# Gate and up projections of a hybrid decoder block: most 512-column matmuls become pairs of 256 columns

## The chip, the cores and the metric

The kernel runs on one core of one Trainium2 chip. The metric is the device time of one execution in microseconds (us). Its engines are called PE (TensorE, the matmuls), DVE (VectorE), ACT (ScalarE), POOL (GpSimd) and SP (SyncE, which issues the DMAs here); PEld is PE's weight load, which overlaps its matmuls.

## The reference

One layer of a decoder block with D = 2048, 256 tokens and a hidden width of 5632. Four token mixers share an input and an output projection; behind them comes a gated feed-forward part with a short causal convolution over the gate. The change lies in the first half of that part, the two projections by `w_gate` and `w_up`:

```python
def conv_ffn(h, w_gate, w_up, conv_w, conv_b, w_down):
    gate = causal_dwconv(h @ w_gate, conv_w) + conv_b
    return (jax.nn.silu(gate) * (h @ w_up)) @ w_down
...
        h = rmsnorm(x, norm_ffn[l]) * (1.0 + sc2) + sh2
        x = x + g2 * conv_ffn(h, ffn_w_gate[l], ffn_w_up[l], ffn_conv_w[l], ffn_conv_b[l], ffn_w_down[l])
```

All of it is float32.

## The kernel before

The kernel computes a float32 product as three products of fp32r parts. Each operand is split into a high part (the value rounded to fp32r) and a low part (what is left): `x w` becomes `xh wh + xl wh + xh wl`. The weights are split as they arrive. `load` (L153) brings a piece of 128 x 1024 values by one DMA on SP's queue into `wr` (five buffers), and `load_split` (L158) makes `wh` by a cast on ACT (L115) and `wl` by a subtraction on DVE (L116, recorded at L100), three buffers of each. All matmuls go through `mm` (L97).

The order of the program is: the modulation vectors and the input projection (tiles `acc` and `ext`), the mixers (`gdt`, `oxt`), the output projection (`wot`), then the feed-forward part (`fpt`). One form of the earlier stages is spoken of below: in the input projection, `gdn` uses each weight tile twice, once with the 256 columns of the high half of the activations and once with the 256 of the low half, both into the same columns of `acc`, and then the `wl` tile with the high half.

In the feed-forward part the normalized activations stand in `H2` (a buffer named `bigA` in the profile): for each of the 16 K tiles of 128 rows, 512 columns, of which the first 256 are the high half of the 256 tokens and the last 256 the low half. `proj` (L1026) makes 512 output features of the gate or of the up projection. It takes four banks of PSUM from the pool `fpp`, which has eight, one bank for each column tile of 128 features, and goes over the 16 K tiles in eight loads of two. For each K tile there are four matmuls of 512 columns (`wh` of a column tile with both halves of `H2`; the sum with the high half arrives in the bank's columns 0 to 255, that with the low half in 256 to 511) and four of 256 columns (`wl` with the high half, added into columns 0 to 255). At the end ACT copies the second half of each bank to `lo` (L1040), and DVE adds it to the first half in place (L1041).

The loop at L1045 calls `proj` for the gate and for up, 11 times each, so there are 88 loads for the gate and 88 for up. The results stay in PSUM; behind each pair, ACT and DVE apply the convolution, the SiLU and the product, and split the result into `AH` and `AL`. From these the down projection is made, with `AH` and `AL` as the weights and the pieces of `w_down` as what streams, in chunks of 512 and 256 columns.

The instructions of each engine are put in order by a scheduler that works ahead of time with an own simulation of the engines. So the order on PE is not quite that of the source: at the start of a gate projection, where banks of PSUM come free one by one, it goes by column tile over several K tiles, and the 512- and 256-column matmuls come in pairs or alternate.

Of the kernel before, what the change touches and what calls it, by code (L numbers as in the profile page):

```python
# [8 lines left out]
F32 = mybir.dt.float32  # L9
# [3 lines left out]
ALU = mybir.AluOpType  # L13
# [3 lines left out]
P = 128  # L17
D = 2048
KT = D // P
T = 256  # L20
# [53 lines left out]
def trunk_kernel(ctx: ExitStack, tc: tile.TileContext, x, c, w_mod, b_mod, norm_mix, norm_ffn, w_in,  # L74
# [4 lines left out]
    V, S_, G, PE = nc.vector, nc.scalar, nc.gpsimd, nc.tensor  # L79
# [16 lines left out]
    def mm(o, l, r, start=True, stop=True):  # L96
        PE.matmul(o, lhsT=l, rhs=r, start=start, stop=stop, skip_group_check=True)  # L97

    def tt(o, a, b, op):
        V.tensor_tensor(out=o, in0=a, in1=b, op=op)  # L100
# [57 lines left out]
    def load_split(view, k0, nk, c0, n):  # L158
        wr = load(view, k0, nk, c0, n)
        wh = wp.tile([P, 1024], F32R, name="wh", tag="wh", bufs=3).rearrange("p (k n) -> p k n", n=n)  # L160
        wl = wp.tile([P, 1024], F32R, name="wl", tag="wl", bufs=3).rearrange("p (k n) -> p k n", n=n)
        split(wh[:, 0:nk], wl[:, 0:nk], wr[:, 0:nk])
        return wh, wl
# [64 lines left out]
    with ExitStack() as ph:  # L228
# [59 lines left out]
        with ExitStack() as st:  # L288
# [19 lines left out]
            b = ext()  # L308
            PE.transpose(b[:, 0:KT], crow, ident[:KT, :KT])
            act(cond, b[:, 0:KT], AF.Silu)  # L310
            b = ext()
# [11 lines left out]
            for k in range(0, KT, 2):  # L323
                b = ext().rearrange("p (k t) -> p k t", t=T)
# [653 lines left out]
        with tc.tile_pool(name="op", bufs=2, reuse_waits="tile") as op:  # L978
            for n, (c0, w) in enumerate(chunks):
                ns, gs = slice(c0, c0 + w), slice(c0 % 1024, c0 % 1024 + w)  # L980
                a = a0
                if n > 0:
                    a = [wop.tile([P, 512], F32, name="wot", tag="wot")[:, 0:w] for _ in range(NT)]
# [8 lines left out]
    with ExitStack() as ph:  # L992
        fpp = ph.enter_context(tc.tile_pool(name="fpp", bufs=8, space=PSUM, reuse_waits="tile"))
        fpt = lambda: fpp.tile([P, 512], F32, name="fpt", tag="fpt")
        H2 = bigA()
        with tc.tile_pool(name="hp", bufs=2, reuse_waits="tile") as hp:
# [9 lines left out]
            for k in range(0, KT, 2):  # L1006
                b = fpt().rearrange("p (k t) -> p k t", t=T)
# [17 lines left out]

        def proj(gp, view, c0):  # L1026

            a = [fpt() for _ in range(4)]
            for g in range(KT // 2):
                wh, wl = load_split(view, 2 * g, 2, c0, 512)  # L1030
                for kk in range(2):
                    k = 2 * g + kk
                    fs = lambda f: slice(f * P, f * P + P)
                    for f in range(4):
                        mm(a[f], wh[:, kk, fs(f)], H2[:, k], start=k == 0, stop=False)
                    for f in range(4):
                        mm(a[f][:, 0:T], wl[:, kk, fs(f)], H2[:, k, 0:T], start=False, stop=k == KT - 1)
            for b in a:
                lo = gp.tile([P, T], F32, name="lo", tag="lo")
                S_.copy(lo, b[:, T:])  # L1040
                tt(b[:, 0:T], b[:, 0:T], lo, ALU.add)  # L1041
            return [b[:, 0:T] for b in a]

        with tc.tile_pool(name="gp", bufs=2, reuse_waits="tile") as gp:
            for n in range(NF // 4):  # L1045
                gt = proj(gp, wg_v, 512 * n)
                ut = proj(gp, wu_v, 512 * n)
                for i in range(4):
                    f = 4 * n + i
                    w3 = lambda j: V3[:, j * NF + f:j * NF + f + 1]  # L1050
                    cv = gp.tile([P, T], F32, name="cv2", tag="cv2")
                    act(cv, gt[i], AF.Identity, scale=w3(2), bias=CB[:, f:f + 1])
                    for sh in (1, 2):
                        stt(cv[:, sh:], gt[i][:, 0:T - sh], w3(2 - sh), cv[:, sh:], ALU.mult, ALU.add)
                    act(cv, cv, AF.Silu)
                    tt(cv, ut[i], cv, ALU.mult)
                    split(AH[:, f], AL[:, f], cv)
# [4 lines left out]
        with tc.tile_pool(name="op2", bufs=1, reuse_waits="tile") as op:  # L1062
            chunks = ((0, 512), (512, 512), (1024, 512), (1536, 256), (1792, 256))
            fs = op.tile([P, NT, len(chunks)], F32, name="fs")
            f1 = op.tile([P, 4], F32, name="f1")
            for n, (c0, w) in enumerate(chunks):
# [3 lines left out]
                a = [fpt()[:, 0:w] for _ in range(NT)]  # L1070
                nk = 1024 // w
                for g in range(NF // nk):
                    wh, wl = load_split(wd_v, nk * g, nk, c0, w)
                    for kk in range(nk):
                        k = nk * g + kk
# [55 lines left out]
```

## Time and profile before

| | |
|---|---|
| time, median of 3 runs | 1303.85 us (1300.9 to 1304.77) |
| profiled execution: its time | 1303.01 us |
| profiled execution: span of the core | 1301.2 us |
| mean granted TensorE clock | 0.985 |
| PE busy | 1248.5 us, 7927 matmuls |
| PEld busy | 1091.0 us |
| DVE busy | 891.0 us |
| ACT busy | 636.7 us |

The time is that of the execution as the device reports it, the span the distance from the first to the last instruction in the trace. Where an engine is named with a tile (`fpt<-bigA,wh`), the tile written stands ahead of the arrow and the tiles read behind it. The shape behind that is partitions x columns. "128*128" is the part of the array in use. In a row of groups, busy time and the mean of one instruction follow, then the idle time of the engine just before them and what ended it. In a row of the timeline the first number is the start in us from the start of the span, the second the length of the row, and xN the number of instructions that were merged in it.

### The profile page before, as it was taken

The page shows a single profiled execution, that of the slowest core. Times are in us where ns is not written, and L with a number is a line of the kernel's source. Part 1 is how long each engine was busy: PE and PEld are TensorE (multiplying, and loading weights), DVE is VectorE, ACT ScalarE, POOL GpSimd, SP SyncE. Part 2 cuts the span into 40 slices and gives each one's busy share as a digit, 9 for nine tenths or more (in the row PEclk, how much of TensorE's full clock was granted, in tenths as well). Part 3 has the DMA queues.
Part 4 walks back from the last instruction along what each step waited for, and adds up shares of the span by engine and source line. Part 5 has one row for each costly group of instructions (what it writes and reads, how often), then busy time and mean ns, then how long its engine had stood idle before and what let it go on. Part 6 is the DMA issues. An engine that isn't in the chain of part 4 may idle for free.

```text
span 1301.2 us, 20372 instructions
## 1 busy us (share of the span) xinstructions
PE 1248.5 (96%) x7927; PEld 1091.0 (84%) x7927; DVE 891.0 (68%) x1201; ACT 636.7 (49%) x1000; POOL 22.7 (2%) x31
## 2 busy tenths in 40 slices
PE   2799999999999999999999999999999999999996
PEld 1799999898876788888888888888888888888896
DVE  7689797989763397676656656665656597964543
ACT  3455344774354454564545555554555454443432
POOL 0200000010000100000000000000000000000000
PEclk9799999999999999999999999999999999999998
DMA  9999998796566988556576666666665699875652
GB/s 321 277 367 378 337 341 290 259 339 212 164 236 240 318 317 276 156 165 192 163 214 190 186 187 193 190 172 206 187 187 163 219 374 359 323 243 194 192 181 81
DMA packets 174231, 311.94 MB, mean 240 GB/s; under 512 B 16172, under 2 KB 65331, under 8 KB 173495
## 3 DMA queue, kind: packets, MB, share of 16 engines
q1 hardware_dynamic: 174135, 310.65, 72.9%
q8 instruction: 62, 1.02, 0.3%
q14 instruction: 34, 0.28, 0.1%
HBM read 308.51 MB, written 2.10 MB: 239 GB/s over the span
## 4 chain that ended last, share of the span: by engine, by line
PE 92%; DMA 4%; SPq 1%; DVE 1%; ACT 1%; issue 1%; POOLq 0%; ACTq 0%; DVEq 0%
PE fpt L97 57%; PE ext L97 16%; PE wot L97 5%; PE gdt L97 4%; PE acc L97 4%; PE bgt L97 3%; DMA wm<-in_w_mod_dram 3%; PE oxt L97 2%; DMA wr<-in_w_in_dram 1%; DVE ga L103 1%; DMA ct<-in_cst_dram 0%; ACT xT L1011 0%; DVE wl L100 0%; SPq L399 0%; SPq L155 0%
## 5 line engine op out<-in xcount | busy, mean ns | idle before, releaser
L100 DVE TENSOR_TENSOR wl<-wr,wh 128x1024 fp32r<-128x1024 f32 x384 | 469.2, 1223 | 293.6 <-ACT wh L115 292.6
L115 ACT CAST wh<-wr 128x1024 fp32r<-128x1024 f32 x384 | 403.4, 1051 | 494.9 <-PE fpt L97 310.8
L97 PE MATMUL fpt<-bigA,wh 128*128 128x512 f32 x1408 | 399.6, 395 | 2.1 <-DVE bigA L103 2.1
L97 PEld LDWEIGHTS fpt<-bigA,wh 128*128 128x128 f32 x1408 | 239.3, 189 | 32.8 <-issue 2.2
L97 PEld LDWEIGHTS fpt<-bigA,wl 128*128 128x128 f32 x1408 | 222.4, 188 | 34.4 <-DVE wl L100 3.6
L97 PE MATMUL fpt<-bigA,wl 128*128 128x256 f32 x1408 | 240.4, 279 | 0.0
L103 DVE SCALAR_TENSOR_TENSOR ga<-wm,cond,ga 128x1024 f32<-128x1024 f32 x139 | 177.8, 1279 | 9.5 <-DMA wm<-in_w_mod_dram 8.6
L97 PE MATMUL fpt<-wl,AH 128*128 128x512 f32 (+1 forms) x440 | 152.9, 348 | 0.0
L97 PE MATMUL fpt<-wh,AL 128*128 128x512 f32 (+1 forms) x440 | 152.5, 347 | 0.0
L97 PE MATMUL fpt<-wh,AH 128*128 128x512 f32 (+1 forms) x440 | 142.5, 348 | 0.0
L97 PE MATMUL ext<-bigA,wh 128*128 128x256 f32 x768 | 137.0, 280 | 0.0
L97 PEld LDWEIGHTS ext<-bigA,wh 128*128 128x128 f32 x768 | 117.3, 188 | 3.1 <-DVE dS L100 0.8
L97 PE MATMUL ext<-bigA,wl 128*128 128x256 f32 x384 | 107.2, 280 | 1.7 <-DVE wl L100 1.7
L97 PEld LDWEIGHTS fpt<-wh,AH 128*128 128x128 f32 x440 | 83.3, 189 | 10.7 <-issue 0.2
L97 PEld LDWEIGHTS fpt<-wh,AL 128*128 128x128 f32 x440 | 83.3, 189 | 10.5 <-issue 0.2
L97 PEld LDWEIGHTS fpt<-wl,AH 128*128 128x128 f32 x440 | 83.3, 189 | 10.5 <-issue 0.2
L97 PE MATMUL acc<-bigA,wh 128*128 128x256 f32 x384 | 70.3, 289 | 4.7 <-ACT bigA L115 2.9
L97 PEld LDWEIGHTS ext<-bigA,wl 128*128 128x128 f32 x384 | 72.1, 188 | 3.0 <-DVE wl L100 2.1
L97 PE MATMUL ext<-wh,bigA 128*128 128x256 f32 (+1 forms) x320 | 68.0, 304 | 0.0
L97 PEld LDWEIGHTS acc<-bigA,wh 128*128 128x128 f32 x384 | 60.7, 198 | 5.1 <-ACT bigA L115 3.0
L97 PE MATMUL wot<-wh,bigA 128*128 128x512 f32 (+1 forms) x256 | 63.2, 337 | 0.0
L97 PEld LDWEIGHTS ext<-wh,bigA 128*128 128x128 f32 x320 | 51.7, 188 | 5.5 <-ACT wh L115 1.7
(340 smaller groups left out, 1191.9 us busy)
## 6 DMA issues: line engine op xcount, KB each, us to landing
wm<-in_w_mod_dram SPq DMA_DIRECT2D x192, 512.0 KB, 5.8
wr<-in_w_in_dram SPq DMA_DIRECT2D x88, 512.0 KB, 9.7
wr<-in_ffn_w_gate_dram SPq DMA_DIRECT2D x88, 512.0 KB, 3.9
wr<-in_ffn_w_up_dram SPq DMA_DIRECT2D x88, 512.0 KB, 4.4
wr<-in_ffn_w_down_dram SPq DMA_DIRECT2D x88, 512.0 KB, 4.5
wr<-in_w_out_dram SPq DMA_DIRECT2D x32, 512.0 KB, 4.2
xt<-in_x_dram SPq DMA_DIRECT2D x2, 1024.0 KB, 7.2
bigC<-in_x_dram SPq DMA_DIRECT2D x2, 1024.0 KB, 8.6
```

The lines of the kernel that those rows point to most:

```text
L97: PE.matmul(o, lhsT=l, rhs=r, start=start, stop=stop, skip_group_check=True)
L100: V.tensor_tensor(out=o, in0=a, in1=b, op=op)
L103: V.scalar_tensor_tensor(out=o, in0=a, scalar=s, in1=b, op0=op0, op1=op1)
L115: S_.copy(hi, src)
```

## The change

`proj` alone changes. In each load of two K tiles only column tile 0 of the first K tile keeps its matmul of 512 columns. Every other `wh` tile is used in two matmuls of 256 columns, one with the high and one with the low half of `H2`, and both add into columns 0 to 255 of the bank. The matmuls with `wl` stay as they are. So only the bank of column tile 0 has anything in its second half, and only that bank is followed by the copy to `lo` and the add.

```diff
             a = [fpt() for _ in range(4)]
             for g in range(KT // 2):
                 wh, wl = load_split(view, 2 * g, 2, c0, 512)
                 for kk in range(2):
                     k = 2 * g + kk
                     fs = lambda f: slice(f * P, f * P + P)
                     for f in range(4):
-                        mm(a[f], wh[:, kk, fs(f)], H2[:, k], start=k == 0, stop=False)
+                        if f == 0 and kk == 0:
+                            mm(a[f], wh[:, kk, fs(f)], H2[:, k], start=k == 0, stop=False)
+                        else:
+                            mm(a[f][:, 0:T], wh[:, kk, fs(f)], H2[:, k, 0:T], start=k == 0, stop=False)
+                            mm(a[f][:, 0:T], wh[:, kk, fs(f)], H2[:, k, T:], start=False, stop=False)
                     for f in range(4):
                         mm(a[f][:, 0:T], wl[:, kk, fs(f)], H2[:, k, 0:T], start=False, stop=k == KT - 1)
-            for b in a:
-                lo = gp.tile([P, T], F32, name="lo", tag="lo")
-                S_.copy(lo, b[:, T:])
-                tt(b[:, 0:T], b[:, 0:T], lo, ALU.add)
+            lo = gp.tile([P, T], F32, name="lo", tag="lo")
+            S_.copy(lo, a[0][:, T:])
+            tt(a[0][:, 0:T], a[0][:, 0:T], lo, ALU.add)
             return [b[:, 0:T] for b in a]
```

## The prediction

> **What bounds the kernel now.** First the page: busy time by engine, then the chain that ended last by engine and line.
>
> ```profile
> span 1301.2 us, 20372 instructions
> ...
> PE 1248.5 (96%) x7927; PEld 1091.0 (84%) x7927; DVE 891.0 (68%) x1201; ACT 636.7 (49%) x1000; POOL 22.7 (2%) x31
> ...
> PE 92%; DMA 4%; SPq 1%; DVE 1%; ACT 1%; issue 1%; POOLq 0%; ACTq 0%; DVEq 0%
> ```
>
> PE carries 92% of the chain. The chain in order of time shows that gate and up and the down projection after them are one unbroken stretch of PE:
>
> ```profile
> 549.25 738.94 PE fpt L97 x4141
> ```
>
> So in gate and up only what changes PE's own pace, or makes PE wait, moves the end. The groups by line and shape of that stage (549 to 1042 us):
>
> ```profile
> L97 PE MATMUL fpt<-bigA,wh 128*128 128x512 f32 x1408 | 399.6, 395 | 2.1 <-DVE bigA L103 2.1
> L97 PE MATMUL fpt<-bigA,wl 128*128 128x256 f32 x1408 | 240.4, 279 | 0.0
> L97 PEld LDWEIGHTS fpt<-bigA,wh 128*128 128x128 f32 x1408 | 239.3, 189 | 32.8 <-issue 2.2
> L97 PEld LDWEIGHTS fpt<-bigA,wl 128*128 128x128 f32 x1408 | 222.4, 188 | 34.4 <-DVE wl L100 3.6
> L100 DVE TENSOR_TENSOR wl<-wr,wh 128x1024 fp32r<-128x1024 f32 x175 | 214.1, 1224 | 175.3 <-ACT wh L115 175.3
> L115 ACT CAST wh<-wr 128x1024 fp32r<-128x1024 f32 x176 | 184.6, 1049 | 198.7 <-PE fpt L97 188.1 <-ACT bigA L112 5.5 <-issue 2.6
> ```
>
> Three things are seen here. There is one weight load for each matmul. PE's waits sum to some 8 us of 493, 2.1 of them the start of the stage. And ACT waits 188 us for PE to free a `wh` buffer, which is what a bound PE looks like from the other side. A mean of 395 ns is not the pace: matmuls overlap, and the pace is the distance of their starts. That is read from the timeline of PE, here a clean stretch of ten K tiles:
>
> ```profile
> 620.52 1.09 PE L97 MATMUL fpt<-bigA,wh 128*128 128x512 f32 x4
> 621.45 0.62 PE L97 MATMUL fpt<-bigA,wl 128*128 128x256 f32 x4
> 621.91 1.09 PE L97 MATMUL fpt<-bigA,wh 128*128 128x512 f32 x4
> 622.84 0.62 PE L97 MATMUL fpt<-bigA,wl 128*128 128x256 f32 x4
> ...
> 634.39 1.09 PE L97 MATMUL fpt<-bigA,wh 128*128 128x512 f32 x4
> ```
>
> From 620.52 to 634.39 are ten K tiles: 1.387 us each. The four 512-column matmuls take 0.93 of it (232.5 ns each), the four 256-column ones 0.45 to 0.46 (0.457 by difference, 114 ns each). Two of 256 columns cost 228 ns, less than one of 512. This is the core of the case, since the change trades the one for the other.
>
> **What the change does, part by part.** There are 88 + 88 loads of two K tiles. In each, one of eight 512-column matmuls stays and seven become two 256-column ones with the same weights: 1232 matmuls of 512 columns go, 2464 of 256 come, and with them 1232 more weight loads, as each matmul has its own. Columns streamed are the same. A load's block on PE is now 2 x 1.387 = 2.774 us. Afterwards it is one 512-column matmul and 14 + 8 = 22 of 256.
>
> The price of a 256-column matmul in such a long row is the unknown. The trace of before has rows of the very form in the input projection (`wh` with the high half, `wh` again with the low half, then `wl`, into the same columns), and they do not agree:
>
> ```profile
> 114.17 0.39 PE L97 MATMUL acc<-bigA,wh 128*128 128x256 f32 x2
> 114.40 0.28 PE L97 MATMUL acc<-bigA,wl 128*128 128x256 f32 x1
> ...
> 116.89 0.62 PE L97 MATMUL acc<-bigA,wh 128*128 128x256 f32 x4
> ```
>
> ```profile
> 168.40 0.40 PE L97 MATMUL acc<-bigA,wh 128*128 128x256 f32 x2
> 168.64 0.28 PE L97 MATMUL acc<-bigA,wl 128*128 128x256 f32 x1
> ...
> 170.64 0.40 PE L97 MATMUL acc<-bigA,wh 128*128 128x256 f32 x2
> ```
>
> 114.17 to 116.89 holds 24 matmuls: 113.3 ns each. 168.40 to 170.64 holds 19: 117.9. Same code, same stage; the pace stays one or the other for long runs. A third pace stands in the 256-column chunks of the down projection, where the weights are `AH` and `AL` and what streams is `wh` or `wl`:
>
> ```profile
> 1224.12 0.39 PE L97 MATMUL fpt<-wh,AL 128*128 128x512 f32 x1
> ...
> 1225.02 0.40 PE L97 MATMUL fpt<-wh,AH 128*128 128x256 f32 x2
> 1225.25 0.28 PE L97 MATMUL fpt<-wl,AH 128*128 128x256 f32 x1
> ...
> 1226.45 0.28 PE L97 MATMUL fpt<-wh,AH 128*128 128x256 f32 x1
> ```
>
> There ten take 1.20 us: 120 ns each, and four of 512 before them 0.90: 225 ns by these rounded starts. None of it is the clock, as the table by stage shows (columns: stretch, its length, PE's busy time, PEld's, granted clock, DMA share, GB/s):
>
> ```profile
> 138.00:154.00 16.00, 16.00 (x143) 16.00 (x142) 1.00 1.08 361
> 168.00:208.00 40.00, 40.00 (x342) 40.00 (x342) 1.00 1.04 356
> 552.40:593.50 41.10, 41.10 (x237) 35.88 (x236) 1.00 0.59 168
> 1228.00:1286.00 58.00, 58.00 (x486) 58.00 (x485) 1.00 0.45 137
> ```
>
> I take 113.3, since the 256-column matmuls of the stage itself, with its own operands and right behind its 512-column ones, go at 114, nearest to it. The first four after the 512 I leave at their 0.457 in all, the other 18 at 113.3 (2.040), the 512 at its mean of 0.2325: 2.729 us. Against 2.774 that is 45 ns less, times 176 loads: 7.8 us less.
>
> Second, the interleaved places. At the start of a gate projection the order on PE is by column tile, and the 512- and 256-column matmuls alternate:
>
> ```profile
> 644.09 0.39 PE L97 MATMUL fpt<-bigA,wh 128*128 128x512 f32 x1
> 644.32 0.28 PE L97 MATMUL fpt<-bigA,wl 128*128 128x256 f32 x1
> 644.44 0.40 PE L97 MATMUL fpt<-bigA,wh 128*128 128x512 f32 x1
> ...
> 647.97 0.40 PE L97 MATMUL fpt<-bigA,wh 128*128 128x512 f32 x1
> ```
>
> Eleven pairs take 3.88 us, 353 ns each against 347 in the clean stretch. These are column tiles with no 512-column matmul afterwards, so the extra 6 ns goes: 12 pairs by ten projections, 0.7 us.
>
> Third, the end of a projection. `lo` and its add go for three column tiles of four:
>
> ```profile
> L1040 ACT COPY lo<-fpt x88: 359/372/378, 576.6 to 1045.8; 128x256 f32<-128x256 f32 x88
> L100 DVE TENSOR_TENSOR fpt<-fpt,lo x88: 418/423/427, 577.8 to 1047.1; 128x256 f32<-128x256 f32 x88
> ```
>
> 66 of 88 go: 24.6 us of ACT and 27.9 of DVE. They run beside PE's matmuls of the next projection, so I cost them at nothing but for one wait. Behind each gate projection's interleaved start PE waits for a `wl`, ten times, and the clean stretch before it shows no such wait:
>
> ```profile
> PEld fpt L97 <- DVE wl L100: 3.6, 10, 0.4
> ...
> 603.66 1.10 PE L97 MATMUL fpt<-bigA,wh 128*128 128x512 f32 x4
> 604.69 0.74 PE L97 MATMUL fpt<-bigA,wl 128*128 128x256 f32 x4
> 605.27 0.62 PE L97 MATMUL fpt<-bigA,wh 128*128 128x512 f32 x2
> ```
>
> 603.66 to 605.27 is 1.61 us instead of 1.387: some 0.2 us, 2 us in ten. The last column tiles run late there because PSUM is freed by the chain of copies, adds and activations, they hold the `wh` buffers, and so the next split is late. With the chain shorter, half of it, 1.0 us, is my guess between 0 and 2. If the cover went, and ACT's and DVE's work did not fit beside PE, each would still have over 170 us of waiting in the stage.
>
> DMA is at a share of 0.59 here and the loads, their order and size stay. The instructions that PE has to be fed come faster (one matmul in 119 ns instead of 174), but the input projection keeps 113 at a DMA share over 1, so I cost this at nothing.
>
> Sum: 7.8 + 0.7 + 1.0 = 9.5 us. The profiled execution took 1303.0 us (span 1301.2), 0.8 below the median of 1303.85. 1303.0 - 9.5 = **1293.5 us**. This case by itself reaches from 1290.5 (the 512-column matmul at 226, all of the wait gone) to 1296 (neither of the wait nor of the interleaving).
>
> **Rivals.**
>
> *The long row settles into the slower pace* (ends slower). Place: the 22 matmuls after each 512. A run at 117.9 held from one load to the next in the input projection, and the rows of 168 to 208 us show how long. Block: 0.2325 + 22 x 117.9 = 2.826 us, 52 ns over 2.774, times 176 = 9.2 us more, less 1.7 from the other two terms: 1310.5. It decides from a mean pace of (2774 - 232.5) / 22 = 115.5 ns up. For it: no stretch of before has 22 in a row in this stage, and half of the input projection runs so. Against: the four at 114 here, and one 512 in each block gives the pace a new start.
>
> *A fixed price for each matmul* (ends slower too). In the down projection 225 for 512 and 120 for 256 read as some 15 ns for each matmul beside its columns; two of 256 then cost 240. Block: 232.5 + 22 x 120 = 2.873, 99 ns more, 17.3 us, less 1.7: 1318.6. Against: here 512 costs 232.5 and 256 costs 114, which leaves no fixed price, so I give it little. The Trainium skill ("TensorE: Matmul & The Clock Gate", Back-to-back issue gap) states such a price: N / 2.4 plus about 2.5 ns warm. By that rule the 1232 added matmuls would cost an estimated 3 us, some 1306, within what counts as no change. The trace here disagrees on both sizes, 232.5 against the rule's estimated 215.8 and 114 against 109.2.
>
> *Both paces by turns.* With half of the blocks at each, the mean is 115.6: the first term is near zero, the other two remain, 1302: no change.
>
> *Nothing on PE, a new wait instead.* Were PE made to wait for a split at each of the 22 ends of projections by 0.5 us more, 11 us would eat the gain: 1304. Against: ACT and DVE only lose work.
>
> **How the numbers follow.** About 0.3% (3.9 us) is what can be told from no change: 1299.9 and 1307.8. The quick pace 0.60, the slower pace 0.17, the fixed price 0.07, both paces by turns 0.11, a new wait 0.05. Faster: 0.60 and a little of the mixed case, 0.63. Same: most of the mixed case and of the waits, 0.14. Slower: 0.23. The range goes from 1290.5 to 1310.5, which takes in the slower pace's own value; outside lies the fixed price and half of what spreads around that pace.
>
> **What would show it.** In the timeline of PE a block should take 2.72 to 2.73 us, with 256-column starts 113 to 114 ns apart. At 2.82 the second pace, at 2.87 the third. The stage ends now with the first matmul of the down projection:
>
> ```profile
> 1041.94 0.39 PE L97 MATMUL fpt<-wh,AH 128*128 128x512 f32 x1
> ```
>
> From 549.25 that is 492.7 us; it should be 483. `lo` should count 22, and PE's wait for `wl` at most ten short ones. The down projection should keep its pace; if its 512-column matmuls change theirs, that is outside this sum and would make it wrong, as would a new wait of PE behind the projections.

## The result: slower by 0.43%, and the profile after

The changed kernel takes 1308.42 us (median of 8 runs, 1306.49 to 1311.78), the kernel before 1302.68 us (8 runs, 1300.17 to 1304.79). The ratio is 1.0043, 95% interval 1.0028 to 1.0058. The prediction was 1293.5 and "faster"; the range, up to 1310.5, still holds the time, but the forecast direction is wrong.

The page of the profile after, the same lines as before. This execution took 1306.49 us:

```profile
span 1304.7 us, 22649 instructions
...
PE 1252.8 (96%) x9159; PEld 1152.3 (88%) x9159; DVE 871.1 (67%) x1135; ACT 615.8 (47%) x934; POOL 22.6 (2%) x31
...
PE 92%; DMA 4%; DVE 1%; ACT 1%; SPq 1%; issue 0%; POOLq 0%; ACTq 0%; DVEq 0%
```

PE has 1232 matmuls and as many weight loads more; DVE and ACT are some 20 us less busy each. PE still carries 92% of the chain, and the stage is still one stretch of PE:

```profile
547.92 743.74 PE fpt L97 x5373
```

The timeline of PE after, two blocks of two K tiles each. A row names the form of its first matmul, so the row "128x512 x7" is the 512 and six of 256 columns:

```profile
700.52 1.11 PE L97 MATMUL fpt<-bigA,wh 128*128 128x512 f32 x7
701.47 0.63 PE L97 MATMUL fpt<-bigA,wl 128*128 128x256 f32 x4
701.94 1.11 PE L97 MATMUL fpt<-bigA,wh 128*128 128x256 f32 x8
702.88 0.64 PE L97 MATMUL fpt<-bigA,wl 128*128 128x256 f32 x4
703.35 1.11 PE L97 MATMUL fpt<-bigA,wh 128*128 128x512 f32 x7
...
706.18 1.11 PE L97 MATMUL fpt<-bigA,wh 128*128 128x512 f32 x7
...
1045.38 0.39 PE L97 MATMUL fpt<-wh,AH 128*128 128x512 f32 x1
```

From 700.52 to 706.18 two blocks take 5.66 us, 2.83 each, where 2.73 was forecast and 2.774 stood before. Eight of 256 columns take 0.94 (701.94 to 702.88) and four take 0.47: 117.5 ns each by these rounded starts, 117.8 by the unrounded ones. That is the slower of the two paces that the trace of before had shown in the input projection. From 547.92 to the first matmul of the down projection at 1045.38 the stage takes 497.5 us against 492.7 before. Behind it the down projection keeps its time, 259.3 us to the end of the span in both.

What the change was to save it did save. `lo` counts 22, as foreseen, and PE's ten waits for `wl` are gone: no row of the view of waits from 549 to 1045 us has PE or its weight load waiting.

```profile
L1044 ACT COPY lo<-fpt x22: 360/360/365, 573.3 to 1046.1; 128x256 f32<-128x256 f32 x22
```

### The profile page after: what moved, and what is told of

Read it like the earlier page. It is cut to its first block, busy times and chain, and to the rows that moved or that the text cites. A ratio compares the mean times of both kernels' runs of the same rounds, so it can differ in the third digit from the quotient of the medians.

```text
span 1304.7 us, 22649 instructions
## 1 busy us (share of the span) xinstructions
PE 1252.8 (96%) x9159; PEld 1152.3 (88%) x9159; DVE 871.1 (67%) x1135; ACT 615.8 (47%) x934; POOL 22.6 (2%) x31
## 4 chain that ended last, share of the span: by engine, by line
PE 92%; DMA 4%; DVE 1%; ACT 1%; SPq 1%; issue 0%; POOLq 0%; ACTq 0%; DVEq 0%
PE fpt L97 57%; PE ext L97 15%; PE wot L97 5%; PE acc L97 5%; PE gdt L97 4%; PE bgt L97 3%; PE oxt L97 2%; DMA wr<-in_w_in_dram 2%; DMA wm<-in_w_mod_dram 2%; DMA wr<-in_w_out_dram 1%; DVE ga L103 1%; DVE wl L100 0%; ACT wh L115 0%; DMA ct<-in_cst_dram 0%; ACT xT L1011 0%
## 5 line engine op out<-in xcount | busy, mean ns | idle before, releaser
L97 PE MATMUL fpt<-bigA,wh 128*128 128x256 f32 (+1 forms) x2640 | 399.9, 289 | 2.1 <-DVE bigA L103 2.1
L97 PEld LDWEIGHTS fpt<-bigA,wh 128*128 128x128 f32 x2640 | 354.9, 189 | 10.4 <-issue 2.2
L97 PEld LDWEIGHTS fpt<-bigA,wl 128*128 128x128 f32 x1408 | 196.7, 189 | 0.0
```

## What the experiments were for

The question is what sets the pace of the 256-column matmuls, 113.3 ns (quick) or 117.8 (slow). From here on "a 512" and "a 256" are matmuls of so many columns, and "pace" is the time from one start to the next. The single 512s of the changed kernel give a hint. In its trace one 512, at 553.9 us, comes upon the quick pace: it takes 226 ns, and the 256s behind it go at 117.8; before, four 512s in a row (226, 236, 231, 236 by the starts in the trace) were followed by 118, 113, 114, 113. Theory A: the pace is a state of PE. One 512 by itself throws it from the quick into the slow pace, an even number back to back leaves or brings it into the quick one, and 256s keep what they find. The rivals: long rows of 256s are slow anyway (B), neighbours with the same weights or the same PSUM bank are slow (C), or the number of 512s in a block decides and not their place (D). Ratios are against runs of the kernel before on the same chip.

### No 512 at all

```diff
-                        if f == 0 and kk == 0:
+                        if False:
...
-            lo = gp.tile([P, T], F32, name="lo", tag="lo")
-            S_.copy(lo, a[0][:, T:])
-            tt(a[0][:, 0:T], a[0][:, 0:T], lo, ALU.add)
```

> No 512-column matmul at all: every wh tile goes in two matmuls of 256 columns, and no bank has a lo copy and add. The clean block of two K tiles is then 24 matmuls of 256. Theory A (parity): the pace is a state of PE; one 512-column matmul by itself throws PE from the quick pace (113.3 ns) into the slow one (117.8), two back to back bring it back, and 256-column matmuls keep whatever state they are in. With no 512 the pace has nothing that changes it and stays what it was at the start of the stage or after the last pause: mostly one pace for hundreds of matmuls, block 2.72 us or 2.83 us, time 1293 or 1306. Theory B (long rows): any long row of 256-column matmuls in this stage settles at 117.8, so 2.83 us throughout and about 1307. Theory C (same weights or bank twice running costs more): the wh pairs pay and the wl ones do not, so wh starts near 119 and wl starts near 113 in the timeline, block about 2.81.

Measured: 1289.61 us median, 3 us under the lower time expected; ratio, of the five runs that lie together, 0.9899 (0.9877 to 0.9921). These five lie between 1284.65 and 1292.55, the sixth at 1305.84. The table by stage of the profiled execution (1289.54 us) shows one pace from end to end; columns as in the prediction's table:

```profile
560.00:1020.00 460.00, 460.00 (x4061) 460.00 (x4061) 1.00 0.66 194
```

460 us for 4061 matmuls, two or three of which began before the window, are 113.3 ns each. B and C fall: no row is longer than this one, and it has all the neighbours with the same weights and bank. The sixth run lies 16 us over the median, and 24 x 4.45 ns x 176 would be 18.8 us. That would fit a state that is kept whichever it is, but that run has no trace, so what made it longer is not shown.

### Two 512s back to back in each block

```diff
-                        if f == 0 and kk == 0:
+                        if f < 2 and kk == 0:
```

(with the copy and add for two banks)

> Two 512-column matmuls back to back at the head of each block (column tiles 0 and 1 of the first K tile), 20 of 256 behind them. Theory A (parity): the second 512 returns PE to the quick pace, so the block is 226 + 236 + 118 + 19 x 113.3 = 2.733 us, 41 ns less than before's 2.774, and with PE's wait for wl gone the time is about 1294 to 1296, faster than both kernels. Theory B (long rows settle at 117.8): 2 x 236 + 20 x 117.8 = 2.83 us, about 1307. Theory C (same weights or bank twice running): between, about 2.80 us, 1303 to 1305.

Measured: 1291.19 us, 3 us under the 1294 to 1296 expected; ratio 0.9918 (0.9901 to 0.9935). One 512 more in each block than the changed kernel, and 17 us less. The timeline:

```profile
701.20 1.08 PE L97 MATMUL fpt<-bigA,wh 128*128 128x512 f32 x6
702.12 0.62 PE L97 MATMUL fpt<-bigA,wl 128*128 128x256 f32 x4
702.57 1.07 PE L97 MATMUL fpt<-bigA,wh 128*128 128x256 f32 x8
703.48 0.62 PE L97 MATMUL fpt<-bigA,wl 128*128 128x256 f32 x4
703.93 1.08 PE L97 MATMUL fpt<-bigA,wh 128*128 128x512 f32 x6
```

The block is 2.73 us (701.20 to 703.93) as theory A gave it, and eight of 256 take 0.91: 113.8.

### Two 512s in each block, apart

```diff
-                        if f == 0 and kk == 0:
+                        if f == 0:
```

> The same number of 512-column matmuls as two back to back, two of a block of 22 matmuls, but apart: column tile 0 of each of the two K tiles, ten and more matmuls of 256 between them. Theory A (parity): each stands alone, so each finds and leaves PE at the slow pace: 2 x 236 + 20 x 117.8 = 2.83 us a block, about 1307, like the changed kernel and 11 us over the kernel with the two back to back. Theory B (long rows): also 2.83. Theory D (it is the number of 512s in a block that matters, not where they stand): the same time as the kernel with the two back to back.

Measured: 1309.58 us, ratio 1.0063 (1.0038 to 1.0087), 18 us over the kernel with the two together. Number, columns and weight loads of the matmuls are the same and only their place differs; beside PE the kernel with the two apart even has one copy and add less per projection. D falls. The timeline has two K tiles, a block, in 2.83 us:

```profile
701.56 1.11 PE L97 MATMUL fpt<-bigA,wh 128*128 128x512 f32 x7
...
702.97 1.11 PE L97 MATMUL fpt<-bigA,wh 128*128 128x512 f32 x7
...
704.38 1.11 PE L97 MATMUL fpt<-bigA,wh 128*128 128x512 f32 x7
```

### Another order among the 256s

```diff
                         else:
                             mm(a[f][:, 0:T], wh[:, kk, fs(f)], H2[:, k, 0:T], start=k == 0, stop=False)
-                            mm(a[f][:, 0:T], wh[:, kk, fs(f)], H2[:, k, T:], start=False, stop=False)
+                    for f in range(4):
+                        if f > 0 or kk > 0:
+                            mm(a[f][:, 0:T], wh[:, kk, fs(f)], H2[:, k, T:], start=False, stop=False)
```

> The changed kernel's single 512 in a block, but with another order of the 256-column ones: for each K tile first all column tiles with the high half, then all with the low half, then wl. No two neighbours have the same weights or write the same bank. Theory A (parity): order among the 256s does not matter, 2.83 us a block, within 2 us of the changed kernel. Theory C (same weights or same bank twice running costs more): the pace goes to 113 to 114, block 2.73 us, time about 1294 to 1297.

Measured: 1309.45 us, ratio 1.0055 (1.0039 to 1.0072), 1 us from the changed kernel, with the 256s of a block at 117.8 ns in the trace. C falls a second time.

### Twenty-two pairs against twenty-two single ones

```diff
-                        if f == 0 and kk == 0:
+                        if f < 2 and k == 0:
```

(with the copy and add for two banks)

> Two 512-column matmuls back to back only at the first K tile of each projection (22 pairs in all); everything else in 256 columns. Theory A (parity): each pair puts PE into the quick pace and nothing takes it out, so all blocks but the first of a projection take 24 x 113.3 = 2.72 us; time about 1288, and every run near it, unlike the kernel without any 512, whose runs lay between 1284.7 and 1305.8. Theory B2 (a row of 256s drifts to the slow pace by and by unless each block has a pair): between 1291 and 1305.

```diff
-                        if f == 0 and kk == 0:
+                        if f == 0 and k == 0:
```

> One 512-column matmul only at the first K tile of each projection (22 in all); everything else in 256 columns. It differs from the kernel with a pair there by 22 matmuls of some 4200. Theory A (parity): the first single one throws PE to the slow pace and the later ones leave it there, so a block takes 24 x 117.8 = 2.83 us, time about 1305 to 1307. Rival: so few 512s can't matter, so the time is that of the kernel with the pairs, about 1288.

Measured: with the pairs 1291.25 us (1290.54 to 1293.01), ratio 0.9909 (0.9894 to 0.9923); with the single ones 1309.03 us (1304.99 to 1312.49), ratio 1.0037 (1.0025 to 1.0048). 22 of some 4200 matmuls decide on 18 us. The pairs' time is 3 us over the 1288 expected, and the single ones' 2 us over 1305 to 1307; the four runs of the pairs lie together, as expected. By its time alone B2 ("between 1291 and 1305") would still stand; the stage table decides against it. The stage tables, of the kernel with the pairs and then of that with the single ones:

```profile
580.00:1020.00 440.00, 440.00 (x3842) 438.30 (x3842) 1.00 0.65 195
```

```profile
560.00:570.00 10.00, 10.00 (x90) 10.00 (x90) 1.00 0.64 183
580.00:1040.00 460.00, 460.00 (x3888) 459.06 (x3887) 1.00 0.63 187
```

With the pairs, 440 us hold 3842 matmuls, 40 of them of 512 columns: 113.3 ns for a 256, with no drift over the 188 between two pairs. With the single ones, the first projection is still quick behind its start (10 us for 90, two or three of them from before the window, 114). So the first lone 512 did not do what theory A said of it; it ran at a granted clock of 0.50, as the stage did up to 557.7 us, and why that matters is not shown. From the second projection's 512 on, at 573.7 us, all is slow, and the later ones don't bring the quick pace back (460 us for 3888, with 20 of 512: 118 ns for a 256).

### Half of the change

```diff
-                        if f == 0 and kk == 0:
+                        if kk == 0:
```

(with the copy and add for all four banks)

> Half of the change: the first K tile of each load keeps its four 512-column matmuls, the second goes in 256 columns. Theory A (parity): four back to back are an even number, as in the kernel before, so the 12 + 4 matmuls of 256 run at the quick pace: 929 + 118 + 15 x 113.3 = 2.75 us a block, time about 1294 to 1297. Rival (every 512 changed for two of 256 costs the same as in the whole change): half of its loss, 1304 to 1305.

Measured: 1298.7 us (1295.47 to 1299.68), ratio 0.9958 (0.9944 to 0.9972): a gain, as theory A has it, where half of the whole change's loss would have been 1304 to 1305. The median is 2 us above the 1294 to 1297 expected; the profiled execution took 1295.94. Its timeline has the block at 2.75 us:

```profile
700.33 1.09 PE L97 MATMUL fpt<-bigA,wh 128*128 128x512 f32 x4
701.26 0.62 PE L97 MATMUL fpt<-bigA,wl 128*128 128x256 f32 x4
701.72 1.07 PE L97 MATMUL fpt<-bigA,wh 128*128 128x256 f32 x8
702.63 0.62 PE L97 MATMUL fpt<-bigA,wl 128*128 128x256 f32 x4
703.08 1.09 PE L97 MATMUL fpt<-bigA,wh 128*128 128x512 f32 x4
```

### The state switched on purpose

```diff
+            wide = {0: (4, 2), 3: (8, 1), 7: (8, 2)}.get(c0 // 512, (-1, 0)) if view is wg_v else (-1, 0)
...
-                        if f == 0 and kk == 0:
+                        if k == wide[0] and f < wide[1]:
```

> All in 256 columns but for five matmuls in the stage: a pair of 512s back to back in the first gate projection (K tile 4), one alone in the fourth (K tile 8), a pair in the eighth (K tile 8). Theory A (parity): the starts are 113.3 ns apart from the first pair on, 117.8 from the single one on, through four gate and four up projections, and 113.3 again from the last pair on; time some 7 us over the kernel with a pair at each projection's start, about 1295. Rival (the pace hangs on operands, loads or the other engines' work): no change of pace at these three places.

One execution: 1294.81 us. The stage table, ahead of the single 512, between it and the last pair, and behind that pair:

```profile
600.00:680.00 80.00, 80.00 (x709) 80.00 (x708) 1.00 0.68 196
700.00:860.00 160.00, 160.00 (x1361) 160.00 (x1360) 1.00 0.64 186
890.00:1020.00 130.00, 130.00 (x1149) 130.00 (x1149) 1.00 0.68 195
```

80 us for 709, 160 for 1361, 130 for 1149; with the two or three of each that began before the window taken off, 113.3, 117.8 and 113.4 ns. And the two places in the timeline:

```profile
689.17 0.62 PE L97 MATMUL fpt<-bigA,wl 128*128 128x256 f32 x4
689.63 1.10 PE L97 MATMUL fpt<-bigA,wh 128*128 128x512 f32 x7
690.56 0.63 PE L97 MATMUL fpt<-bigA,wl 128*128 128x256 f32 x4
...
870.05 0.63 PE L97 MATMUL fpt<-bigA,wl 128*128 128x256 f32 x4
870.52 1.09 PE L97 MATMUL fpt<-bigA,wh 128*128 128x512 f32 x6
871.45 0.62 PE L97 MATMUL fpt<-bigA,wl 128*128 128x256 f32 x4
```

Nothing else changes there: same operands, granted clock 1.00, about the same DMA share. One instruction makes all of the next 1534 slower, and two in a row undo it. This is one execution, but the first half of it is found throughout: in the traces of the changed kernel and of the experiments a lone 512 comes upon the quick pace at a granted clock of 1.00 in 26 places, and behind all 26 the pace is slow.

### Three, four, and narrower ones

```diff
+            kind = (("", "3", "2", "4", "apart", "2", "128", "2", "384", "2", "")[c0 // 512] if c0 else "first") if view is wg_v else ""
...
+                        if k == 8 and f == 0 and kind == "384":
+                            mm(a[f][:, 0:384], wh[:, kk, fs(f)], H2[:, k, 0:384], start=False, stop=False)
+                            mm(a[f][:, P:T], wh[:, kk, fs(f)], H2[:, k, 384:], start=False, stop=False)
+                        elif k == 8 and f == 0 and kind == "128":
+                            mm(a[f][:, 0:P], wh[:, kk, fs(f)], H2[:, k, 0:P], start=False, stop=False)
+                            mm(a[f][:, P:T], wh[:, kk, fs(f)], H2[:, k, P:T], start=False, stop=False)
...
```

> All in 256 columns but for one event in each gate projection, at its K tile 8 (the first at K tile 4), the up projections without any: a pair of 512s; three in a row; a pair; four in a row; two apart (K tiles 8 and 9); a pair; one 256-column matmul as two of 128; a pair; one 512 as one of 384 and one of 128; a pair. Theory A (parity of the 512s that stand back to back, from the quick pace): starts 113.3 ns apart behind the pairs and behind the four; 117.8 behind the three and behind the two apart, up to the next pair. For the narrow forms theory A says nothing; if the change of pace needs a matmul that lasts two slots of 113 ns with one weight load, then the two of 128 leave the pace as it is. Rival (only a 512 alone is harmful, any row of two or more is good): 113.3 behind the three.

One execution: 1296.01 us. Behind the three the pace was slow, behind the two apart too; behind the four and behind four of the five pairs quick, and both narrow forms were quick again within seven matmuls. But the pair that followed the three did not bring the quick pace back:

```profile
604.77 0.62 PE L97 MATMUL fpt<-bigA,wl 128*128 128x256 f32 x4
605.22 1.09 PE L97 MATMUL fpt<-bigA,wh 128*128 128x512 f32 x5
606.15 0.64 PE L97 MATMUL fpt<-bigA,wl 128*128 128x256 f32 x4
...
649.96 0.64 PE L97 MATMUL fpt<-bigA,wl 128*128 128x256 f32 x4
650.43 1.09 PE L97 MATMUL fpt<-bigA,wh 128*128 128x512 f32 x6
651.36 0.63 PE L97 MATMUL fpt<-bigA,wl 128*128 128x256 f32 x4
651.84 0.87 PE L97 MATMUL fpt<-bigA,wh 128*128 128x256 f32 x6
```

The four that came next stood in this slow pace and did bring the quick one back. So theory A holds for what a row of 512s does to the quick pace (one or three: slow; two: quick; four: quick too, by the kernel before and the half of the change), but the slow pace behind three is not the same state as that behind one: "slow" has more than one form.

It does not hold in full for a lone 512 in the slow pace either. Most leave it slow, but in 13 of some 760 places the quick pace follows: once in the changed kernel, twice in the kernel with two apart, ten times in the half of the change, where 512s stand one by one at the start of a gate projection. The place in the changed kernel:

```profile
549.41 1.10 PE L97 MATMUL fpt<-bigA,wh 128*128 128x256 f32 x8
550.35 0.63 PE L97 MATMUL fpt<-bigA,wl 128*128 128x256 f32 x4
550.82 1.09 PE L97 MATMUL fpt<-bigA,wh 128*128 128x256 f32 x7
...
552.20 1.07 PE L97 MATMUL fpt<-bigA,wh 128*128 128x256 f32 x8
553.11 0.62 PE L97 MATMUL fpt<-bigA,wl 128*128 128x256 f32 x4
```

Eight 256s take 0.94 us from 549.41 and 0.91 from 552.20; between them stands one 512, the fourth of the seven from 550.82. The next lone 512, at 553.9, ends the quick pace again.

And the instructions of the stage alone don't set the pace that it starts with. The last two kernels have the same 50 matmuls of 256 columns ahead of their first pair. Behind the first few, these go at 113 ns in the trace of the kernel with the switch and at 118 in that of this one (one execution each, on two chips):

```profile
549.53 1.07 PE L97 MATMUL fpt<-bigA,wh 128*128 128x256 f32 x8
550.44 0.62 PE L97 MATMUL fpt<-bigA,wl 128*128 128x256 f32 x4
```

```profile
551.99 1.10 PE L97 MATMUL fpt<-bigA,wh 128*128 128x256 f32 x8
552.93 0.63 PE L97 MATMUL fpt<-bigA,wl 128*128 128x256 f32 x4
```

What in PE the state is, these runs don't say.

## Why the prediction was wrong, step by step

- *PE bounds the stage, and its pace of starts is what counts.* Right: every result above is read from that one view.
- *Two of 256 cost less than one of 512.* Right at the quick pace (226.7 against 232.5), wrong at the slow one (235.6). All in 256 columns runs at 0.99 of the time before. The Trainium skill ("Perfetto Trace Analysis", Matmuls) says that larger matmuls are more efficient where possible; the runs here disagree at the quick pace, 1289.61 us against 1301.14 on the same chip, and agree at the slow one.
- *The long row goes at 113.3.* This is the step that failed. It was taken from the four 256s at 114 in the stage itself, "right behind its 512-column ones". They stood behind four 512s in a row, an even number. The change leaves one. The same step named the first rival's weakness as "one 512 in each block gives the pace a new start"; the switch above shows that a single 512 ends the quick pace, and in the trace after the later ones leave it slow in 173 of 174 places. 22 x 4.45 ns and a 512 at 236 instead of 232.5 make the block 2.827 us: 9.3 us more in 176, where 7.8 less were put down.
- *Interleaving and the wait for `wl`.* Right in sign. The waits went entirely, about 2 us and not 1.0. The 0.7 of the interleaving was misread: 353 ns is, by the unrounded starts, a 512 at 235 and a 256 at 118, the slow pace behind a lone 512. So the rows that the prediction shows already held the sign, and it took it for a price of the order. In the sum the 0.7 stays, since the change makes these places, slow before, no slower.
- *Left out:* the first ten matmuls of the stage run at a granted clock of 0.54 in the profile of before, and not in that of after. The table by stage, before and then after:

```profile
549.00:552.40 3.40, 3.15 (x10) 0.54 0.00 0
```

```profile
548.00:551.40 3.40, 3.40 (x27) 1.00 0.02 5
```

Six of 512 and four of 256 columns should take 1.85 us and take 3.15: some 1.3 us of the two executions' difference that the change did not make, as far as can be told (four of the experiments had such a start too: the other order among the 256s, the pairs and the single ones at each projection's start, and half of the change).

The sum as it should have been: 9.3 - 2.0 - 0.7 - 1.3 = 5.3 us; the two stages differ by 4.8 us, the two medians by 5.7. The first rival had the price (1310.5) and was given 0.17, but not the mechanism: it laid the slow pace to the long row, and the longest row of all, that without any 512, runs at 113.3. Its threshold, a mean of 115.5 ns, fits. The range of the case itself was added up wrongly: with the 512 at 226 and all of the wait gone, 1293.5 becomes 1291.4 and not 1290.5. DVE and ACT lost some 20 us each and not 27.9 and 24.6; neither changes the result.

## What to carry to other kernels

Read a pace at the place and behind the neighbours that the changed code will have: two rows of the same form with two paces can mean a state, and the question is then what sets it, not which row is nearer. In a stage like this one, a dense row of 256-column products with one weight load each, a lone 512 is to be avoided; here a pair at the start of each projection gives 0.9909 of the time before, with its four runs within 2.5 us. A change that looks neutral in work can move some 18 us of 1300 by 22 of some 4200 matmuls, so the distance of starts on PE is worth a look before and after each reordering.

## What the runs showed of the hardware that was not expected

- Streams of fp32r matmuls of 256 columns, each with its own weight load, have two steady paces on the same code, 113.3 and 117.8 ns from start to start, at a granted clock of 1.00. A pace lasts for thousands of matmuls (4061 at 113.3 in one window), and one matmul of 512 columns changes it from quick to slow (26 of 26 places).
- In the quick pace a single 512 takes 226 ns, as two of 256 do, but those behind it take 4.45 ns more each for as long as the state lasts: 6.8 us by this count over the 1534 of the switch experiment.
- Ahead of the first 512 of the stage the same matmuls went at 113 ns in one execution and at 118 in another, on another chip. Whether this is why the six runs of the kernel without any 512 reach from 1284.65 to 1305.84 us is not shown, since one of them alone has a trace.
